# A decoder layer on one core: eight raw weight buffers instead of four, and steps put in another order at the front's end and in the tail

## The chip, the core and the metric

The kernel runs on one core of a Trainium2 chip. A core has five engines, each with its own queue: TensorE (PE in the profile, its weight loads PEld), VectorE (DVE), ScalarE (ACT), GpSimd (POOL) and SyncE (SP), which here issues nearly all transfers from the chip's memory (HBM) to the core's on-chip memory. Matrix products end in eight banks of PSUM. An engine works its queue off in order and waits on semaphores for what another engine or a transfer has to deliver. The metric is the device time of one execution in microseconds; lower is better.

## The reference

One decoder layer for 256 tokens of width 1024, in float32:

```
n = rmsnorm(h);  proj = n @ W_in            # 5136 columns, split into 10 parts
o_a = gla(q, k, v, log_a)                   # gated linear attention, chunks of 64
y_a = (rmsnorm(o_a) * silu(g_r)) @ W_branch_a
o_b = diff_attention(rope(q), rope(k), v)   # causal, 4 heads, two softmaxes each
y_b = (rmsnorm(o_b) * (1 - lambda_init)) @ W_branch_b
h1 = h + (sigmoid(gate_a) * y_a + sigmoid(gate_b) * y_b) @ W_out
n2 = rmsnorm(h1)
top-1 of 4 groups, then top-2 of its 8 experts (router in full precision)
h2 = h1 + sum_e comb[:, e] * ((silu(n2 @ w_gate[e]) * (n2 @ w_up[e])) @ w_down[e])
e = rmsnorm(p @ w_ple)
out = rmsnorm(h2 + sigmoid(h2 @ w_ple_gate) * e)
```

There are 32 experts with three matrices of 1 MB each, so some 100 MB of the 138 MB that the kernel reads are expert weights.

## The kernel before

**Front.** All products with w_in, the branch matrices and w_out run as a list `units` of 114 units. A unit takes one raw weight tile of 128 x 512, splits it into a high and a low part (`part` and `split`, lines 346 and 244: ACT copies the high part, DVE subtracts to get the low one) and multiplies both 128-token halves with three products each (`mm3`, line 411). Units 0 to 7 are q and k of the linear attention, 8 and 9 the forget gate, 10 to 17 its v, then the differential attention's q, k, v, the output gate, 32 units of branch gates, 16 of the branches (82 to 97) and 16 of w_out (98 to 113). `run` (line 383) emits a unit, keeps three units split ahead and five loaded ahead: `raw_load` (line 340) issues the load of unit i into one of four buffers tagged w_raw, on SP.

Between the units two lanes of generators (`back`, `side`) emit the attention steps: `step` (line 361) advances one, and what the generator yields is the number of units until its next step. `head_steps` (line 750) scales a branch's heads, waits by a yield, and transposes them to oT on TensorE (pt is named poT); `merge_steps` (line 805) does the same for the merged branches (pmT). Before unit 78 all that is left in the lanes is emitted at once (lines 787 to 790).

**Slots.** 22 slots of 1 MB, and a 23rd when the front's weight pool is closed, hold first the front's tensors and then expert weights. `ring` (line 200) is the order in which they come free, `tiles` (line 202) the order in which expert weights are loaded: of each group q of four experts eight tiles "gu" (gate and up) and four "d" (down), at the end quarters of the last down matrices ("dq") and of w_ple_gate ("wg"). In the front every third unit issues half a tile, if the list `fill` holds a free slot; at first `NFREE` = 11 do. `refill` (line 217) issues the rest, in the queue order of SP: after the last unit five tiles and a half that is left over, then one for the 23rd slot, then four each time four are used up.

**End of the front.** The last three w_out units are held until their three weight tiles are there (`out_unit`, line 853). `h1_half` adds the residual on DVE, `h1_turn` transposes h1 on TensorE for the router, `h1_square` sums squares on ACT and uses the product's bank as scratch, `logits` (line 895) multiplies with the router weights into a bank that is freed by the first square. `inv_root` (line 954) makes the norm's factor: a sum on DVE and a power on POOL. `route` (line 992) then runs on DVE for both token halves, and `gather` (line 982) collects the tokens of each expert by products with a one-hot matrix (pxg).

**Experts and tail.** `experts_in(q)` (line 1140) gathers, multiplies with gate and up (tile ph), gates, transposes; down products and the scatter back into the accumulators yp follow. The last two groups' down products are done in quarters of 256 columns (`down`, `scatter`, lines 1254 and 1279), interleaved with the final gate's products (pg), which need h2 = hn in the transposed form (`turn`). hn starts as yp + h1, four adds on DVE at lines 1271 to 1274, behind the last group. The end is a list of steps written out by hand (lines 1383 to 1386): sigmoid on ACT, product and add on DVE, squares, the final norm's `root`, and four stores.

The wrapper `Ordered` (line 50) keeps an engine's instructions in program order where its flag is on; in the expert part the framework may reorder them.

Of the kernel before, what the change touches and what calls it, by code (L numbers as in the profile page):

```python
# [20 lines left out]
P = 128  # L21
# [12 lines left out]
NFREE = NSLOT - 11  # L34
# [29 lines left out]
def kernel(  # L64
# [38 lines left out]
    def col(t, a):  # L103
        return a[:, t:t + 1]
# [95 lines left out]
    ring = list(range(11, NSLOT)) + [2, 5, 3, 6, 8, 7, 4, 9, 10, 1, 0, NSLOT]  # L200
# [138 lines left out]

    def raw_load(i):  # L340
        if i < len(units) and i not in raws and i not in parts and i >= state["i"]:
            src, kc, n, name = units[i][0]
            raws[i] = wst.tile([P, kc, n], F32, tag="w_raw", name=f"{name}_r", bufs=4)
            Y.dma_start(raws[i], src.rearrange("(k p) n -> p k n", p=P))

    def part(i):
        if i < len(units) and i not in parts:
            src, kc, n, name = units[i][0]
            if i == 0:
                x_parts(0, [0])  # L350
            elif i < KC:
                x_parts(i)
            if units[i][3]:
                parts[i] = [wst.tile([P, kc, n], F32R, tag=f"w_{c}", name=f"{name}_{c}") for c in "hl"]
                split(parts[i][0], parts[i][1], raws.pop(i), None)
            else:
                parts[i] = raws.pop(i)
            if i == 0:
                x_parts(0, [1])
# [23 lines left out]
    def run(upto):  # L383
        while state["i"] < upto:
            i = state["i"]
            for a in range(5):
                raw_load(i + a)
                if a < 3:
                    part(i + a)
# [3 lines left out]
            raw_load(i + 5)  # L393
# [356 lines left out]
    def head_steps(b):  # L750
# [9 lines left out]
        if b == 0:  # L760
            yield 5
        oT = slot((7, 4)[b], [2, 4, T], F32R, f"oT{b}")
        oTs[b] = oT
        for t in range(NT):
# [5 lines left out]
            yield 2 - b  # L770
# [34 lines left out]
    def merge_steps(n):  # L805
# [5 lines left out]
        yield 3  # L811
# [14 lines left out]
    accw, held = [], []  # L826

# [22 lines left out]
    def out_mm(t, n, k, ws):  # L850
        mm3(accw[t][n], [a[:, k, t * P:(t + 1) * P] for a in mT], [w_[:, 0, :] for w_ in ws], k == 0, k == KC - 1)

    def out_unit(k, n):
        def f(ws):
# [18 lines left out]
            out_mm(1, 1, 6, w61)  # L873
            for n_ in range(2):
                h1_turn(0, n_)
            out_mm(1, 1, 7, w71)
            h1_half(1, 1)
            for n_ in range(2):
                h1_square(0, n_)
# [6 lines left out]

    state["quiet"] = len(units) - 8
# [3 lines left out]
    refill(2 + len(fill))  # L891
# [9 lines left out]
    for n in range(2):  # L901
        h1_turn(1, n)
    logits(0, 1)
    h1_square(1, 0)
    h1_square(1, 1)
    logits(1, 0)
# [43 lines left out]
    rstd2 = wk.tile([P, NT], F32, name="rstd2")  # L950
    mhalf = wk.tile([P, 1], F32, name="mhalf")
    Q.memset(mhalf, -0.5)

    def inv_root(y, ms):

        V.scalar_tensor_tensor(y, ms[0], EPS, ms[1], ALU.add, ALU.add)
        Q.tensor_tensor(y, y, mhalf, ALU.pow)

    for t in range(NT):
        inv_root(col(t, rstd2), (ss2[:, t, 0:1], ss2[:, t, 1:2]))  # L960
# [31 lines left out]
    def route(t):  # L992
# [20 lines left out]
        for i, _ in enumerate(gather(0, t)):  # L1013
            if i:
                yield from until("pk1")
# [124 lines left out]
    def experts_in(q):  # L1140
# [30 lines left out]
        for h in range(2):  # L1171
            last = q == NQ - 1 and h == 1
            E.on = E.on or last
# [73 lines left out]
    last_ys = []  # L1247
# [20 lines left out]

    first = tiles.index(("gu", NQ - 1, 6))
    hn = slot(slot_of(first - 4), [NT, D], F32, "hn")  # L1270
    for t in range(NT):
        for n in range(2):
            cs = slice(n * 512, (n + 1) * 512)
            V.tensor_tensor(by_rows(hn[:, t, cs]), by_rows(yp[t][n]), by_runs(t, n), ALU.add)
# [108 lines left out]
    for f, *a in ((sig, b00), (mul, b00), (sig, b01), (add, b00), (mul, b01), (sig, b10), (square, b00), (normed, 0, 0, 512), (add, b01),  # L1383
                  (mul, b10), (sig, h0), (sig, h1), (normed, 0, 512, 1024), (square, b01), (add, b10), (mul, h0), (square, b10),
                  (add, h0), (root, 0), (mul, h1), (scaled, 0, 0, 512), (square, h0), (add, h1), (scaled, 0, 512, 1024), (square_v, h1),
                  (root, 1), (normed, 1, 0, 512, V), (finished, 1, 512, 768), (scaled, 1, 0, 512, A), (finished, 1, 768, 1024)):
# [32 lines left out]
```

## Time and profile before

| what | value |
|---|---|
| median of 3 runs | 448.23 us (448.19 to 448.48) |
| the profiled execution's own time | 448.06 us |
| its span from the first to the last instruction | 446.5 us |
| TensorE busy | 407.3 us (91%) |
| DVE, ACT, POOL busy | 218.3, 154.5, 35.7 us |
| transfers | 139.18 MB, mean 312 GB/s |

How to read it: an engine's row gives busy time; what counts is where it waits, and for whom. A line of a timeline shows start, duration, engine, line, operation, what is written <- what is read, sizes, count, and in brackets how long the engine stood idle before it and who ended that. Nearly every operation goes through the wrapper's line 58, so tiles and not lines tell them apart; buffer numbers are left out of tile names. A matmul that is listed with 0.6 us for two may overlap its neighbours: the pace is read from start to start. SPq lines are transfers issued by SP; their duration includes SP's own waiting between the merged ones.

### The profile page before, as it was taken

What the parts mean: (1) busy time and instruction counts of PE and PEld (TensorE: products, weight loads), DVE (VectorE), ACT (ScalarE), POOL (GpSimd) and SP (SyncE); (2) the same over time, 40 slices, a digit from 0 to 9 for tenths busy, and PEclk for the clock granted to TensorE, in tenths of its full rate; (3) what the DMA queues carried; (4) which work ended last, traced back from release to release, by engine and by line L of the source; (5) the groups of instructions that cost most, each with busy time, mean ns of one, the idle gap of its engine ahead of it and who ended that gap; (6) DMA issues with size and microseconds to landing.
All of it is one profiled execution on the core that took longest, in us unless ns stands there. A gap on an engine that the chain in (4) does not pass through costs nothing. (4 is left out here: it accounts for less than half of the span.)

```text
span 446.5 us, 7553 instructions
## 1 busy us (share of the span) xinstructions
PE 407.3 (91%) x2876; PEld 273.0 (61%) x2876; DVE 218.3 (49%) x478; ACT 154.5 (35%) x335; POOL 35.7 (8%) x83
## 2 busy tenths in 40 slices
PE   7999999999998999988898988899997998869990
PEld 4767777778786877868545545445263266436670
DVE  4657765896978468656403121222141163073545
ACT  5748645588555535436000000000010100042334
POOL 7200004000160000001000000000000000000003
PEclk9999999999999999999989999989899799988996
DMA  7688875678878888889599999999999999999502
GB/s 222 175 265 277 286 241 156 226 244 283 289 226 275 278 302 274 287 333 349 188 426 418 420 415 420 418 421 419 418 420 420 423 419 420 382 370 364 206 0 94
DMA packets 47214, 139.18 MB, mean 312 GB/s; under 512 B 7282, under 2 KB 17222, under 8 KB 38088
## 3 DMA queue, kind: packets, MB, share of 16 engines
q1 hardware_dynamic: 46872, 138.35, 84.5%
q8 instruction: 23, 0.38, 0.4%
q10 hardware_dynamic: 144, 0.26, 0.2%
q14 instruction: 15, 0.12, 0.1%
q0 software_dynamic: 160, 0.07, 0.1%
HBM read 137.62 MB, written 1.05 MB: 311 GB/s over the span
## 5 line engine op out<-in xcount | busy, mean ns | idle before, releaser
L58 PE MATMUL ph<-wt,xg 128*32 128x256 f32 x1024 | 61.4, 380 | 1.4 <-DMA wt<-in_w_up_dram 1.4
L58 PEld LDWEIGHTS ph<-wt,xg 128*32 128x32 f32 x1024 | 34.4, 110 | 24.5 <-DMA wt<-in_w_up_dram 1.8
L58 ACT ACTIVATE misc<-ph 128x256 f32<-128x256 f32 x8 | 3.1, 384 | 114.6 <-PE ph L58 114.6
L58 PE MATMUL sg<-sg_h,xT 128*128 128x512 f32 x128 | 40.3, 396 | 0.0
L58 PE MATMUL py<-wt,misc 128*32 128x512 f32 x192 | 32.6, 714 | 6.7 <-DVE misc L58 4.7
L58 PEld LDWEIGHTS pxg<-pq,xh 128*128 128x128 f32 x256 | 29.6, 192 | 5.2 <-issue 2.7
L58 PE MATMUL pxg<-pq,xh 128*128 128x128 f32 x256 | 30.4, 276 | 1.9 <-PEq L1061 1.6
L58 DVE TENSOR_TENSOR sg_l<-sg_r,sg_h 128x512 fp32r<-128x512 f32 x32 | 23.5, 736 | 10.5 <-ACT sg_h L58 10.4
L58 PE MATMUL pg<-wg,h2T 128*128 128x512 f32 x96 | 27.2, 420 | 0.7 <-ACT h2T L58 0.7
L58 PEld LDWEIGHTS sg<-sg_h,xT 128*128 128x128 f32 x128 | 23.4, 188 | 4.3
L58 PE MATMUL sg<-sg_l,xT 128*128 128x512 f32 x64 | 25.3, 395 | 0.1
L58 ACT ACTIVATE sg_h<-sg_r 128x512 fp32r<-128x512 f32 x32 | 19.9, 628 | 14.6 <-DMA sg_r<-in_w_in_dram 8.9
L58 PEld LDWEIGHTS py<-wt,misc 128*32 128x32 f32 x192 | 7.4, 124 | 26.8 <-issue 16.0
L58 DVE TENSOR_TENSOR xg<-pxg,g_exp 128x512 f32<-128x512 f32 x16 | 11.0, 690 | 23.0 <-PE pxg L58 22.7
L58 DVE SCALAR_TENSOR_TENSOR misc<-df,wr 128x128 f32<-128x128 bf16 x16 | 3.9, 288 | 37.1 <-PE phT L58 37.0
L58 PEld LDWEIGHTS pg<-wg,h2T 128*128 128x128 f32 x96 | 17.5, 198 | 7.2 <-issue 2.9
L58 PE MATMUL wo<-wo_h,mT 128*128 128x512 f32 x64 | 20.2, 396 | 1.3 <-ACT wo_h L58 1.3
L58 POOL TENSOR_TENSOR sgs<-hn,rows 128x512 f32<-128x512 f32 x2 | 2.5, 1282 | 229.3 <-DVE hn L58 229.3
L58 PE MATMUL y<-y_h,oT 128*128 128x512 f32 x64 | 20.1, 395 | 0.0
L58 DVE TENSOR_TENSOR wo_l<-wo_r,wo_h 128x512 fp32r<-128x512 f32 x16 | 11.0, 691 | 10.2 <-ACT wo_h L58 9.8
L58 DVE TENSOR_TENSOR y_l<-y_r,y_h 128x512 fp32r<-128x512 f32 x16 | 10.9, 691 | 8.3 <-ACT y_h L58 8.3
L58 PE MATMUL y<-late,misc 128*128 128x512 f32 x32 | 14.9, 608 | 0.0
(312 smaller groups left out, 738.7 us busy)
## 6 DMA issues: line engine op xcount, KB each, us to landing
wt<-in_w_up_dram SPq DMA_DIRECT2D x27, 1024.0 KB, 19.2
wt<-in_w_gate_dram SPq DMA_DIRECT2D x24, 1024.0 KB, 19.8
wt<-in_w_down_dram SPq DMA_DIRECT2D x20, 1024.0 KB, 19.8
wt<-in_w_down_dram SPq DMA_DIRECT2D x24, 512.0 KB, 9.3
wt<-in_w_gate_dram SPq DMA_DIRECT2D x16, 512.0 KB, 5.2
sg_r<-in_w_in_dram SPq DMA_DIRECT2D x32, 256.0 KB, 3.2
wt<-in_w_up_dram SPq DMA_DIRECT2D x10, 512.0 KB, 4.5
wo_r<-in_w_out_dram SPq DMA_DIRECT2D x16, 256.0 KB, 4.7
```

Of the source, the lines that this page charges most:

```text
L58: ins = getattr(self.engine, name)(*args, **kwargs)
```

## The change

1. **Raw buffers.** Slot 20 (NSLOT - 2) becomes four more raw buffers for the whole front (`more`); units alternate in fours between the w_raw tiles and the four pieces of `more`. `run` loads eight units ahead. NFREE falls to 10, slot 20 moves to the end of the ring in front of slots 1 and 0, and the closing refill grows by one. The last unit's split parts go into w_raw buffers.
2. **Yields.** Between scaling and transposes `head_steps` waits five units for branch 0 as before and three for branch 1 (none before); `merge_steps` waits five and four instead of three.
3. **End of the front.** The square of (0,0) is emitted ahead of the transposes of h1, that of (0,1) at the end of the held units; the norm's factor for each half is made inside the router's products (`norm2`), in pieces of sinT and cosT, and no longer behind them. In `route` four gather products of the first half are emitted ahead of the second half's rank, not two.
4. **Tail.** The four adds of hn move into `experts_in` of the last group, before the second half of its products (`own_order`).
5. **Last steps.** The final norm's gain product for rows 128 to 255, columns 0 to 511, moves from DVE (behind the second root) to POOL (before the first root); the first root goes ahead of an add, and the scalings of the first half go behind the square of h0.

```diff
-NFREE = NSLOT - 11
+NFREE = NSLOT - 12
-    ring = list(range(11, NSLOT)) + [2, 5, 3, 6, 8, 7, 4, 9, 10, 1, 0, NSLOT]
+    ring = list(range(11, NSLOT - 2)) + [NSLOT - 1, 2, 5, 3, 6, 8, 7, 4, 9, 10, NSLOT - 2, 1, 0, NSLOT]
...
+    more = slot(NSLOT - 2, [4, 512], F32, "more_r")
+
     def raw_load(i):
...
-            raws[i] = wst.tile([P, kc, n], F32, tag="w_raw", name=f"{name}_r", bufs=4)
+
+            raws[i] = wst.tile([P, kc, n], F32, tag="w_raw", name=f"{name}_r", bufs=4) if (i + 2) // 4 % 2 else \
+                more[:, (i + 2) % 4, :].rearrange("p (k n) -> p k n", k=kc)
             Y.dma_start(raws[i], src.rearrange("(k p) n -> p k n", p=P))
...
-                parts[i] = [wst.tile([P, kc, n], F32R, tag=f"w_{c}", name=f"{name}_{c}") for c in "hl"]
+                tag, bufs = ("w_raw",) * 2 if i == state.get("last") else ("w_h", "w_l"), 4 if i == state.get("last") else None
+                parts[i] = [wst.tile([P, kc, n], F32R, tag=tag[c], name=f"{name}_{'hl'[c]}", bufs=bufs) for c in range(2)]
...
-            for a in range(5):
+            for a in range(8):
                 raw_load(i + a)
...
-            raw_load(i + 5)
+            raw_load(i + 8)
...
-        if b == 0:
-            yield 5
+        yield (5, 3)[b]
...
-            yield 2 - b
+            yield 2
...
-        yield 3
+        yield 5 - n
...
+    rstd2, mhalf = sinT[:, 0, 0:2], cosT[:, 0, 0:1]
+    Q.memset(mhalf, -0.5)
...
+    def norm2(t):
+        inv_root(col(t, rstd2), (ss2[:, t, 0:1], ss2[:, t, 1:2]))
...
             out_mm(1, 1, 6, w61)
+            h1_square(0, 0)
             for n_ in range(2):
                 h1_turn(0, n_)
             out_mm(1, 1, 7, w71)
             h1_half(1, 1)
-            for n_ in range(2):
-                h1_square(0, n_)
+            h1_square(0, 1)
...
-    refill(2 + len(fill))
+    refill(3 + len(fill))
...
     logits(0, 0)
-    for n in range(2):
-        h1_turn(1, n)
+    h1_turn(1, 0)
+    norm2(0)
+    h1_turn(1, 1)
     logits(0, 1)
     h1_square(1, 0)
     h1_square(1, 1)
+    norm2(1)
...
-    for t in range(NT):
-        inv_root(col(t, rstd2), (ss2[:, t, 0:1], ss2[:, t, 1:2]))
...
         for i, _ in enumerate(gather(0, t)):
-            if i:
+            if i > 2:
                 yield from until("pk1")
...
+            if last:
+                own_order()
             E.on = E.on or last
...
+    def own_order():
+
+        hn_.append(slot(slot_of(first - 4), [NT, D], F32, "hn"))
+        for t in range(NT):
+            for n in range(2):
+                cs = slice(n * 512, (n + 1) * 512)
+                V.tensor_tensor(by_rows(hn_[0][:, t, cs]), by_rows(yp[t][n]), by_runs(t, n), ALU.add)
...
-                  (add, h0), (root, 0), (mul, h1), (scaled, 0, 0, 512), (square, h0), (add, h1), (scaled, 0, 512, 1024), (square_v, h1),
-                  (root, 1), (normed, 1, 0, 512, V), (finished, 1, 512, 768), (scaled, 1, 0, 512, A), (finished, 1, 768, 1024)):
+                  (normed, 1, 0, 512), (root, 0), (add, h0), (mul, h1), (square, h0), (add, h1), (scaled, 0, 0, 512), (square_v, h1),
+                  (root, 1), (scaled, 0, 512, 1024), (finished, 1, 512, 768), (scaled, 1, 0, 512, A), (finished, 1, 768, 1024)):
```

More of the change, by code (lines that the diff above doesn't have):

```diff
@@ L826, with inv_root @@
     accw, held = [], []
+    rstd2, mhalf = sinT[:, 0, 0:2], cosT[:, 0, 0:1]
+    Q.memset(mhalf, -0.5)
+    def inv_root(y, ms):
+        V.scalar_tensor_tensor(y, ms[0], EPS, ms[1], ALU.add, ALU.add)
+        Q.tensor_tensor(y, y, mhalf, ALU.pow)
+    def norm2(t):
+        inv_root(col(t, rstd2), (ss2[:, t, 0:1], ss2[:, t, 1:2]))
     ss2 = cst.tile([P, NT, 2], F32, name="ss2")
@@ L885 @@
                           (lambda: fill.extend(range(2))) if (k, n) == (1, 1) else None, True))
+    state["last"] = len(units) - 1
     state["quiet"] = len(units) - 8
@@ L949 @@
     rk = wk.tile([P, NT, NE], F32, name="rk")
[L950 to L957, printed above, removed]
-    for t in range(NT):
-        inv_root(col(t, rstd2), (ss2[:, t, 0:1], ss2[:, t, 1:2]))
     def sm(shape, name, dt=F32):
@@ L1246 @@
         wsl[q] = wk.tile([P, 1], F32, name=f"wsl{q}")
-    last_ys = []
+    last_ys, hn_ = [], []
+    first = tiles.index(("gu", NQ - 1, 6))
+    def own_order():
[4 more added lines that the diff above has]
+                V.tensor_tensor(by_rows(hn_[0][:, t, cs]), by_rows(yp[t][n]), by_runs(t, n), ALU.add)
     def outs_of(c, i):
@@ L1265 @@
         experts_in(q)
[L1269 to L1274, printed above, removed]
+    hn = hn_[0]
     V.on = A.on = E.on = Q.on = True
```

## The prediction

> **What bounds the kernel now.** I read the page first, then the engines' busy times by window, the chain of waits, the queue's and the engines' timelines. On the page (40 slices of 11.16 us) TensorE is the busy engine from the first slice to the last, while the transfers are not full until slice 20.
>
> ```profile
> PE   7999999999998999988898988899997998869990
> ...
> DMA  7688875678878888889599999999999999999502
> ```
>
> Windows cut at the seam show it sharper (columns: length, then busy us and instructions of PE, weight load, DVE, ACT, POOL; TensorE clock, DMA share, GB/s):
>
> ```profile
> 214.00:217.00 3.00, 3.00 (x63) 1.80 (x59) 0.77 (x4) 0.00 (x0) 0.00 (x0) 1.00 0.02 5
> 217.00:388.00 171.00, 154.40 (x1470) 82.24 (x1464) 41.00 (x105) 9.03 (x21) 0.00 (x0) 0.95 1.01 414
> ```
>
> Until 217 us TensorE sets the pace; all 23 slots are then full and the queue stands empty for 3 us. From 217 to 388 the transfers are at a share of 1.01, 414 GB/s. What opens that stream is one event, the end of the first half of expert group 0's products, which frees four slots:
>
> ```profile
> 213.29 7.11 PE L58 MATMUL ph<-wt,xg 128*32 128x256 f32 x128
> ```
>
> ```profile
> 217.39 3.35 SPq L58 DMA_DIRECT2D wt<-in_w_gate_dram  x4
> ```
>
> The chain of waits ends so:
>
> ```profile
> 367.12 19.95 DMA wt<-in_w_up_dram
> ...
> 387.11 2.99 PE ph L58 x25
> ...
> 429.93 6.44 PE pg L58 x28
> ```
>
> The last expert tile lands at 387.07 (367.12 + 19.95); behind it TensorE works through the tail to 436.4. So the time is: front on TensorE to 217, a stream of fixed bytes, a tail on TensorE. A microsecond taken from the front moves the stream and everything behind it, if the same number of tiles is loaded when it opens. An idle engine in the front costs nothing unless TensorE waits for it.
>
> **The raw buffers.** Four more buffers let each raw load go out eight units ahead instead of five, and wait for a split that is long done. Five pays in the front where a load is late:
>
> ```profile
> 25.00 0.63 ACT L58 ACTIVATE gv_h<-gv_r 128x512 fp32r<-128x512 f32 x1 [3.73 <-DMA gv_r<-in_w_in_dram]
> ```
>
> ```profile
> 23.71 0.62 PE L58 MATMUL gv<-gv_h,xT 128*128 128x512 f32 x2
> ...
> 24.40 0.61 PE L58 MATMUL gv<-gv_h,xT 128*128 128x512 f32 x2
> ...
> 27.44 1.03 PE L58 MATMUL pl<-tmp 128*128 128x256 f32 x4
> ...
> 35.72 0.63 PE L58 MATMUL gv<-gv_h,xT 128*128 128x512 f32 x2
> ```
>
> Three products (half a unit) take 24.40 - 23.71 = 0.69. From 24.40 to 35.72 stand 11 halves, 7.6 us, and the four products of pl, at most 1.0; 11.3 passed, so 2.7 were lost behind late loads. A load eight units ahead has 8 x 1.38 = 11 us; the page's median landing of a gate load is 3.2 us:
>
> ```profile
> sg_r<-in_w_in_dram SPq DMA_DIRECT2D x32, 256.0 KB, 3.2
> ```
>
> I take all 2.7. On SP the small loads (gains, bias, lambdas) and the half tiles now stand behind three more raw loads each; none of those waits for a running product after the first units, so nothing queues longer. The price is a slot: tile 10 and those behind it get their slot one place earlier in the ring, and at unit 98 the list of free slots is empty, so one half tile slips to unit 101 and 32 halves instead of 33 go out in the run. The closing refill makes up for it: six whole tiles (16 to 21) where five and a half went before. On SP it now follows the last raw load about three units sooner, so tiles 16 to 18 start some 4 us earlier. Tile 19 waits on SP for the last split out of the new slot; only tiles 20 and 21 queue behind it, and these wait for the last w_out product anyway. Seven tiles at 414 GB/s are 17.7 us from about unit 106 on, done before the first four slots come free. The count at the seam is again 23: cost 0, or up to one tile, 2.5 us, if that cover fails.
>
> **More products ahead of transposes.**
>
> ```profile
> 137.40 0.63 PE L58 MATMUL poT<-ident,osl 128*128 128x128 f32 x4 [0.82 <-DVE osl L58]
> ...
> 140.18 0.66 PE L58 MATMUL poT<-ident,osl 128*128 128x128 f32 x4 [0.77 <-DVE osl L58]
> ...
> 163.84 0.40 PE L58 MATMUL y<-y_l,oT 128*128 128x512 f32 x1
> ...
> 166.82 0.63 PE L58 MATMUL pmT<-ident,sg 128*128 128x128 f32 x4 [0.69 <-DVE sg L58]
> ...
> 168.96 0.62 PE L58 MATMUL y<-y_h,oT 128*128 128x512 f32 x2
> ```
>
> The attention head's two transposes wait 0.82 + 0.77 = 1.6 us for the scaling on DVE. With three more units between them the scaling is over: -1.6. By the yields the second transpose then falls to the flush after unit 77, one unit behind the first; its result is first needed at unit 86, so nothing waits. From 163.84 to 168.96 lie one product (0.23), four halves (2.8) and a transpose (0.4): 5.12 - 3.4 = 1.7 lost, 0.7 of it the merge, the rest raw loads that came late to DVE's queue. Two more units for merge 0 and eight buffers take it: -1.7. Merge 0 ends after unit 96 and is used from 98; merge 1 after 104 and from 106, one unit of 1.38 us of cover in each; if a split is late there, up to 0.6 comes back.
>
> **The end of the front.**
>
> ```profile
> 193.68 0.62 PE L58 MATMUL wo<-wo_h,mT 128*128 128x512 f32 x2
> ...
> 196.64 0.73 PE L58 MATMUL wo<-wo_h,mT 128*128 128x512 f32 x2 [1.26 <-ACT wo_h L58]
> ...
> 201.80 1.05 PE L58 MATMUL pr<-wr,h1T 128*128 128x40 f32 x8 [0.70 <-issue]
> ```
>
> ```profile
> 195.96 0.63 ACT L58 ACTIVATE wo_h<-wo_r 128x512 fp32r<-128x512 f32 x1 [2.56 <-DMA wo_r<-in_w_out_dram]
> ...
> 200.97 0.61 ACT L58 ACTIVATE wo<-xh 128x512 f32<-128x512 f32 x1
> ```
>
> ```profile
> 201.13 1.04 DVE L58 TENSOR_TENSOR xh<-wo,xh 128x512 f32<-128x512 f32 x1 [0.91 <-PE wo L58]
> ...
> 205.38 0.26 DVE L58 SCALAR_TENSOR_TENSOR lg<-pr,rstd,brt 128x40 f32<-128x40 f32 x1
> ```
>
> From the first held product (193.68) to the first routing step (205.38) go 11.7 us. The last w_out load costs TensorE 1.26; the logits' bank is freed only by the square at 200.97, which costs 0.70. Both go: that load is eight ahead, and the square of (0,0) now stands in front of the copies on ACT, ready once its add is done. At least 1.96. Laid out anew: six groups of three products at 0.69 (4.1), two transposes at poT's 0.63 (1.3), four logits and one more transpose (1.1), then ACT alone, a copy and two squares with their sums (0.6 and twice 0.8, my estimate from the 0.61), and the norm step: 8.9, and 8.2 if the transposes overlap their neighbours. The last add (1.04) lies beside the logits. The gain is 2.8 to 3.5; I take 3.0. On POOL the two powers now precede the small masks, which the rank product needs somewhere in the 3.6 us between this step and the gather. With two more gather products ahead of the second rank product, TensorE fills a wait there:
>
> ```profile
> 208.94 0.68 PE L58 MATMUL pxg<-pq,xh 128*128 128x128 f32 x4 [0.27 <-DVE r_em L58]
> ```
>
> Of 0.27 here I take 0.2, since DVE's second one-hot still has to come.
>
> **The tail.**
>
> ```profile
> 394.24 0.38 ACT L58 ACTIVATE ys_last<-pyq 128x256 fp32r<-128x256 f32 x1 [0.69 <-PE pyq L58]
> ```
>
> ```profile
> 392.74 3.95 DVE L58 TENSOR_TENSOR hn<-y,xh 128x512 f32<-128x512 f32 x4
> 396.60 0.42 DVE L58 TENSOR_TENSOR ys_last<-pyq,ys_last 128x256 fp32r<-128x256 f32 x1
> ```
>
> The four adds of hn hold DVE until 396.6, while ACT's half is ready at 394.62; the subtraction and the products behind it wait 2.0 us. The adds move to the last half of group 7, where they wait on DVE for the slot of one of that group's gate tiles; behind them queues only the group's gated product, not due before the last products end at 390.1. -2.0. If they land just ahead of that product instead, 3.95 returns and the tail is 2 slower. Late next would be the last weights: the page's DMA digits end in slice 37 (a 5, 413 to 424 us), over 12 us before TensorE's last product at 436.4, so I give nothing back.
>
> At the very end:
>
> ```profile
> 438.87 0.55 POOL L58 TENSOR_TENSOR ro<-ro,mhalf 128x1 f32<-128x1 f32 x1 [0.93 <-DVE ro L58]
> 441.04 0.93 POOL L58 TENSOR_TENSOR ro<-ro,mhalf 128x1 f32<-128x1 f32 x1 [1.62 <-DVE ro L58]
> ```
>
> ```profile
> 440.88 0.69 DVE L58 TENSOR_TENSOR sgs<-hn,rows 128x512 f32<-128x512 f32 x1
> ```
>
> The product moves from DVE to POOL, and the second power, 0.93 beside that DVE product, should take the 0.55 of the first: 0.4. On ACT a square of the second root no longer stands behind the first scaling, which waits for the first power's end at 439.4: 0.4 more, an estimate. Together -0.8; the two scaled halves go to the output queue some 0.4 later, ahead of the last stores. POOL's product delays the first root by some 0.4, off the end. Bounds -1.2 and +0.3. The Trainium skill ("SBUF — State Buffer", section "Summary: rules for kernel authors") says that a GpSimd operation reading SBUF and a VectorE one with two SBUF inputs block each other, the second waiting for the first. By it the first root may wait for a square on DVE and the gain here would be about 0.4; the 0.93 beside the 0.69 agrees with it.
>
> **The sum.** -2.7 - 1.6 - 1.7 - 3.0 - 0.2 = -9.2 for the front, -2.0 and -0.8 behind: -12.0. The profiled execution took 448.06 us (span 446.5), the median of the runs shown is 448.23, 0.17 above: 448.23 - 12.0 = 436.2.
>
> **Rivals.** First, the clock in the tail:
>
> ```profile
> 400.00:404.00 4.00, 3.72 (x20) 1.70 (x21) 1.82 (x2) 0.37 (x2) 0.00 (x0) 0.50 1.06 376
> ```
>
> ```profile
> 401.93 1.87 PE pyq L58 x16
> ...
> 406.77 1.00 PE pyq L58 x16
> ```
>
> ```profile
> 220.00:230.00 10.00, 7.88 (x47) 2.37 (x40) 2.70 (x7) 0.98 (x2) 0.00 (x0) 0.83 1.01 425
> ```
>
> After a sparse stretch TensorE runs at 0.50; sixteen products take 1.87 instead of 1.00, and a slow stretch of some 5 us costs about 2.5 (an estimate from this ratio). If the shorter wait keeps the clock up, the time is 436.2 - 2.5 = 433.7. Against it: at 220 to 230, waits not much longer than those that remain also drop it (0.83 on the mean). The Trainium skill ("TensorE: Matmul & The Clock Gate", section "Part 1: The HAM clock gate") puts the fall after one idle window of about 3.4 us that runs free of the program; these rows agree, and it leaves the outcome open.
>
> Second, DVE takes over. TensorE's waits were also DVE's time to catch up:
>
> ```profile
> 138.17 1.23 ACT L58 ACTIVATE sg_h<-sg_r 128x512 fp32r<-128x512 f32 x2 [3.18 <-DMA sg_r<-in_w_in_dram]
> ```
>
> Where DVE has no such slack, half of the front's gain returns as waits for splits: 448.23 - 4.6 - 2.8 = 440.8. For it: every scaling, split and merge there passes DVE. Against it: ACT waited 3.18 for data here, and DVE behind it, so late loads made part of the backlog.
>
> Third, the change does not reach the stream: the 23rd tile lands late and eats the shift, leaving the tail alone: 448.23 - 2.8 = 445.4. Against it are the 3 us of empty queue.
>
> Fourth, slower: the four pieces of the new slot are waited for as one tile. Then each load into it waits until the one before has landed, 4 x 3.2 = 12.8 us for eight units of 1.38 (11.0): about 1.8 us for each of 14 rounds, +25, with the gains that do not hang on the buffers some 464. It decides from a landing of 2.75 us on. Against it:
>
> ```profile
> 3.13 0.91 SPq L58 DMA_DIRECT2D xn<-in_x_dram  x2
> ```
>
> Two loads into one tile were issued back to back in 0.91 us.
>
> **How the numbers follow.** Chances: the forecast, 434 to 438, 0.52; the clock stays up 0.20; DVE 0.18; no shift 0.05; slower 0.05. The range reaches from the clock rival with the better ends of the front and the last stores (-2) to the DVE rival with 1 us of doubt in the tail: 431.7 to 441.8. It leaves out the last two cases. A measurement of this kernel tells apart about 0.2%, 0.9 us. Faster by more 0.94, within 0.01, slower 0.05.
>
> **What would show it.** In the changed profile: no wait of ACT for gv_r, sg_r or wo_r above 1 us; no wait before poT and pmT; the first routing step about 8.7 us after the first held product; ph of group 0 starting near 204 and the queue full from 208; the last up tile landing near 378; the subtraction of ys_last 0.4 us behind ACT's half; the last power at 0.55. It is wrong if ph starts later than 207, if the stream has gaps past its start, or if waits for DVE take the place of those for loads.

## The result, and the profile after

The changed kernel takes 435.75 us (median of four runs, 434.67 to 437.42); the kernel before 448.21 (447.92 to 448.48). The ratio is 0.9716 with an interval of 0.9689 to 0.9742: 2.8% faster. The profiled execution of the changed kernel took 436.0 us, its span is 434.4.

The page's busy tenths of TensorE and of the transfers, in 40 slices of 10.86 us:

```profile
PE   8999999999999999999898988898798999889990
...
DMA  7879974778898988896699999999999999999902
```

The transfers are full from the same slice on, the 21st, but it begins at 217.2 us (20 x 10.86) and not at 223.2. Windows at the seam (length, busy us and instructions of PE, weight load, DVE, ACT, POOL; clock, DMA share, GB/s):

```profile
206.00:208.00 2.00, 2.00 (x43) 1.19 (x39) 1.69 (x6) 0.00 (x0) 0.00 (x0) 1.00 0.00 0
...
210.00:380.00 170.00, 152.27 (x1458) 82.27 (x1452) 44.93 (x109) 9.01 (x21) 0.00 (x0) 0.97 1.01 416
```

The queue still runs empty before the stream opens, and the stream then holds its share of 1.01 for 170 us. So the number of tiles loaded by then did not shrink, and the shift went through to the end of the stream, as the chain of waits shows:

```profile
360.03 19.60 DMA wt<-in_w_up_dram
379.68 2.99 PE ph L58 x25
```

The last expert tile now lands at 379.63 (360.03 + 19.60) instead of 387.07: 7.4 us earlier. Behind it the tail became shorter by another 4.7.

**Where the time went, stretch by stretch.** I cut each trace at the starts of the same TensorE products: the first product of gv, of dq, of pa (the linear attention's scores, in the middle of dq), of pob (the attention heads' values), of y, of wo, of ph, the last product of ph, the last of pg. Two stretches are left out: pa to pob took 59.23 or 59.24 us in all but tail_only (59.84) and small_first (62.81), and the first to the last ph product took 177.08 to 177.24 in every kernel, which is the stream. The rows below the first two are the experiments; they are told further on.

| kernel | start to gv | gv to dq | dq to pa | pob to y | y to wo | wo to ph | ph to pg | pg to end |
|---|---|---|---|---|---|---|---|---|
| before | 22.22 | 15.12 | 10.20 | 43.47 | 24.67 | 38.39 | 45.60 | 10.50 |
| after | 23.19 | 12.39 | 11.58 | 41.01 | 22.73 | 35.68 | 40.95 | 10.49 |
| after_again | 22.26 | 12.45 | 11.39 | 41.01 | 22.75 | 35.68 | 41.03 | 10.49 |
| buf_only | 22.61 | 12.20 | 11.46 | 41.05 | 22.73 | 38.65 | 45.43 | 10.55 |
| yields_only | 22.35 | 14.90 | 10.40 | 43.59 | 25.47 | 36.02 | 45.61 | 10.48 |
| seam_only | 22.11 | 14.84 | 10.65 | 43.59 | 24.68 | 37.12 | 45.75 | 10.48 |
| tail_only | 23.15 | 15.27 | 10.91 | 44.30 | 24.73 | 37.34 | 42.48 | 10.49 |
| no_yields | 22.30 | 12.77 | 11.03 | 41.07 | 22.73 | 35.68 | 41.02 | 10.49 |
| small_first | 22.20 | 16.64 | 6.84 | 46.27 | 22.59 | 38.48 | 40.96 | 10.50 |
| small_pad | 22.25 | 12.18 | 10.20 | 40.91 | 22.74 | 35.68 | 42.55 | 10.50 |
| route_first | 22.20 | 12.33 | 11.85 | 41.04 | 22.75 | 36.60 | 42.59 | 10.50 |
| root_later | 22.52 | 12.57 | 12.33 | 41.06 | 22.75 | 35.68 | 42.49 | 10.13 |
| before_warm | 22.29 | 15.77 | 11.56 | 43.64 | 25.12 | 37.01 | 45.67 | 10.48 |
| best | 22.19 | 12.18 | 10.19 | 40.91 | 22.75 | 35.68 | 40.94 | 10.14 |

From before to after: +0.97, -2.73, +1.38, -2.46, -1.94, -2.71, then -4.65 and -0.01. Two of these the prediction had not: a loss at the very start and a loss in dq. One caution goes with such differences. In the kernels with five loads ahead two stretches scatter from profile to profile: dq to pa lies between 10.20 and 11.56, and wo to ph, where its order is that of before, between 36.02 and 38.39. The profile of before stands at the low end of the one and at the high end of the other, so what the change did to these two is taken from the experiments and from finer cuts.

The waits that answer to those shown of before, TensorE's timeline first. The heads' transposes wait no more and stand one unit apart:

```profile
139.66 0.60 PE L58 MATMUL poT<-ident,osl 128*128 128x128 f32 x4
141.49 0.60 PE L58 MATMUL poT<-ident,osl 128*128 128x128 f32 x4
...
205.80 7.11 PE L58 MATMUL ph<-wt,xg 128*32 128x256 f32 x128
```

The products of group 0 start at 205.80 instead of 213.29. In dq a wait has come that was not there before; DVE's and TensorE's timelines show it:

```profile
40.61 0.29 DVE L58 TENSOR_TENSOR tmp<-tmp 128x128 f32<-128x128 f32 x1 [3.31 <-DMA tmp<-in_lambda_k_dram]
```

```profile
44.01 0.44 PE L58 MATMUL pq<-ident,gla 128*128 128x128 f32 x2 [0.46 <-DVE gla L58]
```

DVE stands 3.31 us for the last of four small loads (lambda). Behind it in DVE's queue are a split of dq and the factor gla, for which TensorE then waits. In the kernel before the same step ran at nearly the same time:

```profile
40.27 0.29 DVE L58 TENSOR_TENSOR tmp<-tmp 128x128 f32<-128x128 f32 x1 [0.48 <-DMA dq_r<-in_w_in_dram]
```

By the step that reads it, the load is there at nearly the same time, while the products around it have come 1.8 us forward and no longer cover it. SP issued it 1.4 us earlier than before; the queue's timelines, of the changed kernel and of the kernel before:

```profile
34.91 0.43 SPq L58 DMA_DIRECT2D tmp<-in_lambda_k_dram  x1
```

```profile
36.34 0.43 SPq L58 DMA_DIRECT2D tmp<-in_lambda_k_dram  x1
```

So from issue to reader it took 5.7 us (34.91 to 40.61), and before at most 3.9 (36.34 to 40.27).

In the tail the wait of 2.02 us ahead of the products of pz is gone, and sixteen pyq products behind the first gate products take 1.07 us instead of 1.94. TensorE's timeline before and after:

```profile
397.08 0.62 PE L58 MATMUL pz<-ys_last,oT_last 128*128 128x256 f32 x3 [2.02 <-DVE ys_last L58]
...
401.86 1.94 PE L58 MATMUL pyq<-wt,misc 128*32 128x256 f32 x16
403.73 2.11 PE L58 MATMUL pg<-wg,h2T 128*128 128x512 f32 x5
```

```profile
387.24 1.08 PE L58 MATMUL pz<-ys_last,oT_last 128*128 128x256 f32 x4
...
390.44 0.96 PE L58 MATMUL pg<-wg,h2T 128*128 128x512 f32 x3 [0.69 <-ACT h2T L58]
391.33 1.07 PE L58 MATMUL pyq<-wt,misc 128*32 128x256 f32 x16
```

The last steps, POOL's and DVE's together:

```profile
423.32 3.86 POOL L58 TENSOR_TENSOR sgs<-hn,rows 128x512 f32<-128x512 f32 x3 [223.32 <-DVE hn L58]
...
426.09 1.11 DVE L58 SCALAR_TENSOR_TENSOR ro<-sso,sso 128x1 f32<-128x1 f32 x1
...
429.28 0.55 POOL L58 TENSOR_TENSOR ro<-ro,cosT 128x1 f32<-128x1 f32 x1 [1.46 <-DVE ro L58]
```

The first root's step on DVE took 0.15 us in the kernel before:

```profile
438.64 0.15 DVE L58 SCALAR_TENSOR_TENSOR ro<-sso,sso 128x1 f32<-128x1 f32 x1
```

Now it takes 1.11 and ends at 427.20, just when POOL's third product ends (423.32 + 3.86 = 427.18).

### The profile page after: what moved, and what is told of

Same layout as the page of the kernel before. It is cut to its first block, busy times and chain, and to the rows that moved or that the text cites. A ratio compares the mean times of both kernels' runs of the same rounds, so it can differ in the third digit from the quotient of the medians.

```text
span 434.4 us, 7552 instructions
## 1 busy us (share of the span) xinstructions
PE 401.2 (92%) x2876; PEld 275.6 (63%) x2876; DVE 219.5 (51%) x477; ACT 155.4 (36%) x335; POOL 37.1 (9%) x84
## 3 DMA queue, kind: packets, MB, share of 16 engines
HBM read 137.62 MB, written 1.05 MB: 319 GB/s over the span
## 4 chain that ended last, share of the span: by engine, by line
PE 56%; DMA 39%; DVE 2%; issue 1%; ACT 1%; POOL 0%; SPq 0%; POOLq 0%; DVEq 0%
DMA wt<-in_w_down_dram 14%; DMA wt<-in_w_up_dram 14%; PE sg L58 10%; DMA wt<-in_w_gate_dram 9%; PE y L58 6%; PE pg L58 5%; PE wo L58 5%; PE ph L58 3%; PE gqk L58 3%; PE dv L58 3%; PE dk L58 3%; PE gr L58 3%; PE pyq L58 2%; PE pxg L58 2%; DMA dq_r<-in_w_in_dram 1%; PE dq L58 1%
## 5 line engine op out<-in xcount | busy, mean ns | idle before, releaser
L58 PE MATMUL ph<-wt,xg 128*32 128x256 f32 x1024 | 62.5, 380 | 1.8 <-DMA wt<-in_w_up_dram 1.8
L58 PEld LDWEIGHTS ph<-wt,xg 128*32 128x32 f32 x1024 | 35.7, 110 | 24.8 <-DMA wt<-in_w_up_dram 3.1
L58 PE MATMUL py<-wt,misc 128*32 128x512 f32 x192 | 30.9, 656 | 7.4 <-DVE misc L58 4.7
L58 PE MATMUL pg<-wg,h2T 128*128 128x512 f32 x96 | 25.8, 404 | 0.7 <-ACT h2T L58 0.7
L58 PEld LDWEIGHTS sg<-sg_h,xT 128*128 128x128 f32 x128 | 23.4, 188 | 4.4
L58 POOL TENSOR_TENSOR sgs<-hn,rows 128x512 f32<-128x512 f32 x3 | 3.8, 1275 | 223.4 <-DVE hn L58 223.3
L58 PEld LDWEIGHTS pg<-wg,h2T 128*128 128x128 f32 x96 | 16.6, 188 | 6.4 <-issue 2.5
L58 DVE TENSOR_TENSOR sg_l<-sg_r,sg_h 128x512 fp32r<-128x512 f32 x16 | 12.6, 791 | 3.7 <-ACT sg_h L58 3.1
L58 PEld LDWEIGHTS sg<-sg_l,xT 128*128 128x128 f32 x64 | 12.0, 188 | 2.8 <-DVE sg_l L58 0.2
L58 DVE TENSOR_TENSOR sg_l<-more_r,sg_h 128x512 fp32r<-128x512 f32 x16 | 11.7, 743 | 3.9 <-ACT sg_h L58 2.8
L58 PEld LDWEIGHTS y<-y_h,oT 128*128 128x128 f32 x64 | 11.9, 188 | 2.3
```

Of the source, the lines that this page charges most:

```text
L58: ins = getattr(self.engine, name)(*args, **kwargs)
```

## The experiments

The theory after the result: eight buffers take away all waits for raw loads, those before poT and pmT among them; the reordered seam takes away what the buffers would otherwise give back there; the moved adds take 2 us from the tail and the clock the rest; the small loads and POOL's product give something back. The rival for each part is the prediction's own account of it. Each kernel's time is set against runs of the kernel before that stood beside it on the same chip: their medians were 449.37, 448.56 and 449.27 us in the three sets.

**Parts of the change alone, on the kernel before.**

buf_only takes point 1 of the change:

```
-NFREE = NSLOT - 11
+NFREE = NSLOT - 12
...
-            for a in range(5):
+            for a in range(8):
```

> The kernel before with the eight raw buffers alone (the slot taken from the ring, loads eight units ahead, the last parts in the raw buffers, one more tile in the closing refill). The terms as forecast: gv -2.7, the raw loads of the merge stretch -1.0 (1.7 less the 0.7 of the merge), the last w_out load -1.26, together 443.2 us. The rival read from the changed kernel's trace: DVE waits 3.3 us for the lambda loads, which stand on SP as late as before while the products ahead of them have come forward; then 1.4 us of the gv gain return in dq, and the time is 444.6. If the shift never reached the stream it would be 448.2.

Measured: 443.58 us, ratio 0.9885 (0.9847 to 0.9923): a gain of 5.2 us, where the forecast had 5.0 and the rival 3.6. The forecast's number is met by luck. The rival's loss is there (dq to pa 11.46), and the 1.26 of the w_out load does not reach ph; 2.4 in pob to y, which the forecast had given to the yields, make up for both. In the trace gv to dq is 2.9 shorter, pob to y 2.4, y to wo 1.9, with the yields of before. But wo to ph is not shorter (38.65 against 38.39), though the w_out products in it are, by 2.39 (23.41 against 25.80 from the first to the last). What comes forward there is lost behind, as all engines' timeline shows:

```profile
197.57 0.21 POOL L58 MEMSET onesb<- 128x128 bf16 x1 [65.86 <-DMA wt<-in_w_down_dram]
197.57 0.23 DVE L58 SCALAR_TENSOR_TENSOR rstd<-ss 128x1 f32<-128x1 f32 x2 [1.10 <-PE pr L58]
...
198.41 0.10 POOL L58 MEMSET one<- 128x1 f32 x1 [0.64 <-PE pr L58]
...
199.49 0.26 DVE L58 SCALAR_TENSOR_TENSOR lg<-pr,rstd,brt 128x40 f32<-128x40 f32 x1 [1.70 <-POOL rstd L58]
...
201.85 0.19 PE L58 MATMUL pk<-Mb,scr 128*128 128x32 bf16 x1 [2.32 <-DVE r_g L58]
```

In the order of before POOL's masks stand ahead of the norm's powers, and the first mask waits until 197.57. The profile puts that wait down to a transfer. But the norm's step on DVE, which reads only sums of squares, starts at the same 197.57, and there the profile names TensorE's products pr; so what both wait for is most likely memory that the front still holds (no run tests that). The next small step on POOL waits for pr until 198.41. The powers, whose inputs DVE gives at 197.8, come behind these steps, the routing step waits 1.70 for them, and TensorE 2.32 for the routing.

A finer cut shows the price. From the start of the last w_out product to ph it takes 12.58 or 12.59 us in the four kernels with five loads ahead and the old order, 15.24 here, and 12.26 or 12.27 in the changed kernel and in all its variants but route_first. So the seam's reordering is worth more with the buffers than without them.

yields_only takes point 2, seam_only point 3, tail_only the moved adds of point 4:

```
-        if b == 0:
-            yield 5
+        yield (5, 3)[b]
...
-            yield 2 - b
+            yield 2
...
-        yield 3
+        yield 5 - n
```

> The kernel before with the three changed yields alone. As forecast: poT -1.6 and the merge -0.7, 445.9 us, with no wait before poT and pmT. The rival: the raw loads, still five units ahead, are late again wherever TensorE now comes earlier, so that half of it or more returns as waits for gv_r, sg_r or wo_r: 447 or above.

Measured: 449.06 us, ratio 0.9999 (0.9970 to 1.0028), no change. The waits before poT and pmT are gone, and other waits stand in their place, for the splits of late loads (TensorE's timeline):

```profile
139.32 0.73 PE L58 MATMUL sg<-sg_h,xT 128*128 128x512 f32 x2 [0.91 <-ACT sg_h L58]
...
168.48 0.50 PE L58 MATMUL y<-y_l,oT 128*128 128x512 f32 x1 [1.34 <-DVE y_l L58]
```

The rival was right.

```
+            h1_square(0, 0)
             for n_ in range(2):
                 h1_turn(0, n_)
...
-    for n in range(2):
-        h1_turn(1, n)
+    h1_turn(1, 0)
+    norm2(0)
+    h1_turn(1, 1)
```

> The kernel before with the reordered end of the front and the gather alone (squares ahead of the copies, norm steps between the turns, three products of the gather ahead of the second rank product). The wait of 1.26 for the last w_out load stays. As forecast: 3.0 - 1.26 = 1.7 and the gather's 0.2, so 446.3 us. The rival: with the load still late, ACT reaches the squares no earlier and the routing starts where it did, 447.9 or above.

Measured: 448.23 us, ratio 0.9990 (0.9956 to 1.0023): no change that can be told, as the rival had it. In the trace wo to ph is 37.12, 1.3 below before's profile, but the other kernels with five loads ahead have 36.02 to 38.39 in this stretch without that edit, so this difference does not carry it. The finer cut tells more: from the last w_out product to ph it is 12.00 instead of 12.58 or 12.59, so the order alone is worth 0.6, where 1.9 was forecast (1.7 and 0.2).

```
             last = q == NQ - 1 and h == 1
+            if last:
+                own_order()
```

> The kernel before with the four adds of hn moved alone. As forecast: the wait of 2.02 before the last products of pz goes and nothing else, 446.2 us, the granted clock between 396 and 404 still falling to about 0.5. The rival (the clock): the shorter wait leaves TensorE busy enough, the clock stays at 1.00 through the tail, sixteen pyq products take 1.07 instead of 1.94 behind the first gate products, and the time is 443.7.

Measured: 445.03 us, ratio 0.9899 (0.9858 to 0.9939), 4.5 us; in the trace the tail is 3.1 shorter. The wait is gone (2.0), and TensorE's timeline shows a slow clock that begins later and ends earlier than before's (granted clock 0.50 from 400.1 to 403.5, before from 398.4 to 405.2):

```profile
400.12 1.65 PE L58 MATMUL pg<-wg,h2T 128*128 128x512 f32 x3 [0.69 <-ACT h2T L58]
401.70 1.92 PE L58 MATMUL pyq<-wt,misc 128*32 128x256 f32 x16
403.55 1.42 PE L58 MATMUL pg<-wg,h2T 128*128 128x512 f32 x5
```

The next five gate products take 1.42 here and 2.11 in the kernel before. So neither expectation holds whole: more than the wait went, the clock fell all the same, only for a shorter time.

The four ratios multiplied give 0.9774, the whole change has 0.9716; the 0.6% between them (2.6 us, within the intervals' reach) is where buffers and seam work together: from the last w_out product to ph the order takes back 3.0 beside the buffers (15.24 to 12.27) and 0.6 without them. The changed kernel with the old seam, which would test this directly, was not run.

**The changed kernel again, and without the yields.** after_again has no edit; no_yields puts back the three yields of before.

> The changed kernel once more, beside the three below. Its first profile had half-speed products from 7.2 to 11 us (gv 0.97 late) and no fall of the clock behind the last products of pz. If both are a matter of when a window of the clock happens to end, this execution can show another mix: the first gv product between 22.2 and 23.2 us, the tail from the last ph product to the last pg product between 41 and 44 us. If they belong to the kernel, both come again to 0.1 us.

Measured: 435.51 us, ratio 0.9723 (0.9690 to 0.9756). The start to gv is 22.26, so the +0.97 was not the change's. TensorE's timeline in the first profile of the changed kernel, then in this one:

```profile
7.15 1.22 PE L58 MATMUL gqk<-gqk_h,xT 128*128 128x512 f32 x2
...
8.59 1.05 PE L58 MATMUL gqk<-gqk_h,xT 128*128 128x512 f32 x2
```

```profile
7.17 0.73 PE L58 MATMUL gqk<-gqk_h,xT 128*128 128x512 f32 x2 [0.89 <-ACT gqk_h L58]
...
8.24 0.62 PE L58 MATMUL gqk<-gqk_h,xT 128*128 128x512 f32 x2
```

A pair takes 1.05 in one and 0.62 in the other: TensorE was at half pace until some 11 us in the first. Of 14 profiles two, after and tail_only, have this, about 0.95 us each.

> The changed kernel with the three yields of before. By the forecast the waits for the scalings come back before poT (0.8 and 0.8) and pmT (0.7): from the first pob product to the first wo product 2.3 us longer than in the changed kernel, and 2.3 us in all. The rival, from the buffers-only run: those waits came from raw loads that were late to DVE's queue, eight buffers alone remove them, and the yields are worth nothing here: 0.0 to 0.2.

Measured: 435.48 us, ratio 0.9726 (0.9690 to 0.9762), the changed kernel's time. pob to y is 41.07 and y to wo 22.73, within 0.06 of the changed kernel. The yields are worth nothing beside the buffers.

**The small loads.**

```
     def small_loads():
-        yield from wait(6)
+        yield from wait(2)
```

> The changed kernel with the nine small loads four units earlier. If DVE's wait of 3.3 us for the last lambda load is what gives back 1.4 us in dq, that wait is gone, the first pa product comes 11.6 us after the first dq product and not 11.6 later in total: the stretch from the first dq to the first pa product falls from 11.57 to 10.2, and every mark behind it comes 1.4 us earlier. If it was the late dq load itself, the stretch stays at 11.5.

Measured: 446.32 us, ratio 0.9971 (0.9936 to 1.0005): 11 us slower than the changed kernel. The small loads end the first entry of their lane; with it everything that follows in the lane came four units earlier, and the steps no longer meet their data. The largest wait is that of the rotated dq for POOL, 3.07 us (TensorE's timeline):

```profile
76.04 0.66 PE L58 MATMUL pdT<-ident,dqk 128*128 128x128 f32 x4 [3.07 <-POOL dqk L58]
```

The kernel does not answer the question: dq to pa is 6.84, since that lane came forward too. So the edit tested something else than it should. small_pad has it with four empty steps behind the loads:

```
             Y.dma_start(dst, src)
+        yield from wait(4)
```

> The changed kernel with the nine small loads four units earlier as in the run before this, and four empty steps behind them, so that every step that follows in their lane stays where it was. Then only the loads come earlier: if the wait for the last lambda load is what gives back in dq, it is gone, the stretch from the first dq product to the first pa product falls from 11.4 to 11.6 us down to about 10.2, and the end comes 1.2 to 1.4 us earlier, 434.2 us. If dq is held by something else, the stretch stays above 11 and the time near 435.5.

Measured: 434.51 us (433.56 to 434.96), ratio 0.9672 (0.9647 to 0.9697). dq to pa is 10.20, as before the change, and DVE's timeline has the step without a wait, 4.6 us earlier:

```profile
36.04 0.29 DVE L58 TENSOR_TENSOR tmp<-tmp 128x128 f32<-128x128 f32 x1
```

ph of group 0 starts at 203.19, so with this the front gains 10.1. By the traces the small loads' place in SP's queue took 1.2 to 1.4 us of the change's gain, and best, below, has the 10.2 again. The times agree with it (434.51 against 435.5), though the intervals of the ratios still overlap a little.

**The routing step.**

```
-    norm2(1)
     logits(1, 0)
...
-    for _ in range(LAG):
-        next(routes[0])
+    next(routes[0])
+    norm2(1)
+    for _ in range(LAG - 1):
+        next(routes[0])
...
-DUM1, DUM2, DUM3 = 5, 3, 0
+DUM1, DUM2, DUM3 = 2, 3, 0
```

The mask is made behind these steps as well, and the constant one earlier in a piece of cosT.

> The changed kernel with the norm step of the second half of the tokens behind the first routing step on DVE (and on POOL, with the mask and the constant one off POOL's path, and two idle products instead of five). If that norm step, which waits for the last square on ACT, holds the first routing step, it starts about 0.8 us earlier and ph of group 0 with it: from the first ph1T product to the first ph product 12.8 us instead of 13.63, and the end 0.8 earlier. The rival: the first routing step waits for that square anyway, through the memory that it takes over, and nothing moves.

Measured: 436.83 us, ratio 0.9725 (0.9678 to 0.9772), no gain; wo to ph is 0.9 longer. DVE's and TensorE's timelines:

```profile
197.30 0.26 DVE L58 SCALAR_TENSOR_TENSOR lg<-pr,sinT,brt 128x40 f32<-128x40 f32 x1 [1.12 <-PE pr L58]
```

```profile
199.66 0.19 PE L58 MATMUL pk<-Mb,scr 128*128 128x32 bf16 x1 [1.08 <-DVE r_g L58]
199.69 1.63 PE L58 MATMUL idle<-ident 128*128 128x128 f32 x6
201.11 1.91 PE L58 MATMUL pxg<-pq,xh 128*128 128x128 f32 x8
```

The routing step waits for TensorE, 5.83 us after the first transpose of h1 as in the changed kernel (5.80); the norm step held nothing. And with three idle products fewer TensorE stood 1.08 us ahead of the rank product and went on at half pace: six idle matmuls took 1.63 instead of 0.91, eight gather matmuls 1.91 instead of 1.13, 1.5 us together. Two other traces speak for the rival's cause, the memory that the step's output takes over from the front, and against the product that it reads. In buf_only the norm's step, which reads no product, is let go 2.90 us after the first transpose of h1's second half, the routing step here 2.94 after it. And in seam_only, with five loads ahead, the routing step has the product 2.72 after that transpose and does not wait. No run tests it.

**The tail and the end.**

```
-(normed, 1, 0, 512), (root, 0), (add, h0), (mul, h1),
+(normed, 1, 0, 512), (add, h0), (mul, h1), (root, 0),
```

> The changed kernel with the first root two steps later, behind the add and the product of the last two quarters. If that root's small step on DVE was held for about 0.95 us by the product that now runs on POOL, and with it everything behind it on DVE, this takes the hold off the path: from the last pg product to the start of the final two scalings 5.0 us instead of 5.58 to 5.6, 434.9 us. If the wait only moves to the next step on DVE, it stays at 5.5.

Measured: 436.60 us, ratio 0.9719 (0.9691 to 0.9748); the forecast 434.9 is not met. The profile has a slow stretch in the tail (ph to pg 42.49), and the times overlap those of the changed kernel, so I read the end alone. From the start of the last pg product to the final scalings it is 5.09 us (425.87 to 430.95) instead of 5.98, and the step on DVE takes 0.19:

```profile
425.30 3.87 POOL L58 TENSOR_TENSOR sgs<-hn,rows 128x512 f32<-128x512 f32 x3 [224.96 <-DVE hn L58]
429.00 0.19 DVE L58 SCALAR_TENSOR_TENSOR ro<-sso,sso 128x1 f32<-128x1 f32 x1
```

The hold was real: 0.9. The end of the span moves by less, 10.13 against 10.49 from the last pg product: 0.5 is given back between the final scalings and the end. The five stores now go out within 1.5 us (430.59 to 432.13) instead of 2.0; whether that is the reason was not tested.

```
-WARM = 1, 2, 2, 2
+WARM = 1, 2, 6, 2
```

> The kernel before with six idle products instead of two ahead of the last products of pz, inside the 2.02 us in which TensorE waits for DVE there. The wait stays, only the sparse stretch goes. If the tail gained more than the wait because the clock stays up, then here the sixteen pyq products behind the first gate products take 1.07 us instead of 1.94, and from the last ph product to the last pg product it is 43.1 us instead of 45.4 to 45.8, about 2.5 less in the time. If the extra gain came from somewhere else, the stretch stays at 45.6.

Measured: 449.46 us, ratio 0.9989 (0.9957 to 1.0020), no change. TensorE's timeline:

```profile
395.47 1.60 PE L58 MATMUL idle<-ident 128*128 128x128 f32 x12
...
398.48 0.61 PE L58 MATMUL pz<-ys_last,oT_last 128*128 128x256 f32 x3 [1.28 <-DVE ys_last L58]
399.87 1.11 PE L58 MATMUL ph2T<-ident,hn 128*128 128x128 f32 x4 [0.78 <-DVE hn L58]
401.68 1.65 PE L58 MATMUL pg<-wg,h2T 128*128 128x512 f32 x3 [0.69 <-ACT h2T L58]
403.25 1.94 PE L58 MATMUL pyq<-wt,misc 128*32 128x256 f32 x16
```

The idle products filled 0.7 of the wait only; 1.28, 0.78 and 0.69 remain, and the clock falls as before. This neither shows nor refutes that the wait brings the fall; it shows that 2.75 us of waits within 5 us are still enough.

best has the padded small loads, the later root, and two idle products each in the tail's waits of 0.79 and 0.69:

```
-    keep_warm(WARM[2])
+    idle = keep_warm(WARM[2])
     scatter(1, 0)
-    turn(0)
+    for then in (lambda: turn(0), lambda: None):
+        for _ in range(2):
+            E.matmul(idle[:, 0:P], ident, ident, start=True, stop=True)
+        then()
```

> The changed kernel with the padded small loads, the later first root, and two idle products each ahead of the first transposes and the first gate products of the tail, inside TensorE's waits of 0.79 and 0.69 there. If the three causes are right, the sum is 435.5 - 1.3 - 0.6 = 433.6 us, the stretch from the last ph product to the last pg product 41.0 in every run, so that the runs scatter less. If the idle products come later than the data that they wait beside, the tail is 0.1 to 0.3 longer.

Measured: 433.14 us (432.97 to 434.38, five runs), ratio 0.9657 (0.9631 to 0.9682). The interval lies below the changed kernel's, and all five runs lie below the lowest of its eight (434.67). The waits in the tail are 0.34 and 0.24, and pyq takes 1.07, so the clock stayed up in this profile. That is not yet a proof for the idle products, since it stayed up in four of the eight profiles with moved adds and without them too:

```profile
386.45 0.66 PE L58 MATMUL ph2T<-ident,hn 128*128 128x128 f32 x4 [0.34 <-DVE hn L58]
...
387.79 0.96 PE L58 MATMUL pg<-wg,h2T 128*128 128x512 f32 x3 [0.24 <-ACT h2T L58]
388.69 1.07 PE L58 MATMUL pyq<-wt,misc 128*32 128x256 f32 x16
```

## Why the prediction was right, and where it was not

Forecast 436.2, measured 435.75. That the mechanism of the stream is right, a front that ends earlier moves everything behind it, is shown; that the sum came out so closely is luck, because three errors cancel: the front gained 7.5 instead of 9.2 (1.0 of what is missing is the slow start of that one execution), the tail 4.65 instead of 2.0, the end nothing instead of 0.8.

- **gv, -2.7: right.** -2.73 in the changed kernel, -2.9 with the buffers alone.
- **SP's queue, 0: wrong.** The step was that the small loads stand behind three more raw loads each and "nothing queues longer". The last of them was issued 1.4 us earlier, yet its reader started 0.3 later, so it did take longer (5.7 us instead of at most 3.9); and the products that had covered it came earlier, which I did not ask about. The cost is 1.2 to 1.4 us, and small_pad takes it back.
- **poT, -1.6 by the yield: right in sign, wrong in its cause.** The step that failed is that the transposes wait "for the scaling on DVE" and that more units between them are what takes the wait away. DVE's timeline of before shows the second scaling behind a split that waits for ACT, which had waited 3.18 for its load:

```profile
138.84 0.69 DVE L58 TENSOR_TENSOR sg_l<-sg_r,sg_h 128x512 fp32r<-128x512 f32 x1 [0.92 <-ACT sg_h L58]
139.44 0.68 DVE L58 TENSOR_TENSOR osl<-osl,ro 128x512 f32<-128x512 f32 x1
```

  The buffers alone give pob to y 41.05, the yields alone 43.59, before 43.47. The gain was 2.46. I had the row of 3.18 on the table, for the rival on DVE, and did not follow the queue from it to poT.
- **Merge stretch, -1.7: right in size** (-1.94), all of it by the buffers; the 0.7 given to the yields belongs to them too.
- **End of the front and gather, -3.2: 0.5 short.** wo to ph -2.71. From the first held product (188.77) to the first routing step (197.97) it is 9.2, not 8.7. The terms were wrong in size: 2.39 lie in the w_out products, and the buffers alone have that (with five loads ahead these products take 23.4 to 25.8 us from profile to profile, so this part varies); behind the last of them the new order has 12.27 instead of 12.59, a gain of 0.3 where I had 1.9. What I had put at nothing is that the buffers in the old order lose 2.65 there (15.24); the order's worth is to avoid that.
- **DVE takes over (rival): no.** Apart from the load of lambda and TensorE's 0.46 behind it, no wait for DVE came into the units; the backlog was made by the loads, as argued against it.
- **No shift, and four pieces waited for as one tile (rivals): no.** The stream takes 177.1 us in both, and no product waits more than 0.2 us for a split out of the new slot. (The 464 of the last rival kept 1.0 of the merge stretch and the 1.26 of the w_out load, which hang on the buffers too; it should have been 466.)
- **Tail, -2.0, and the clock (rival, 0.20): the rival came, in about half of the profiles.** With the adds behind the last group ph to pg is 45.4 to 45.8 in all five profiles; with the adds moved it is 40.9 to 41.0 in five of nine (best among them, with its idle products) and 42.5 to 42.6 in four. The wait's 2.0 is sure; the clock gives 2.6 or 1.1 on top. I had put it against the rival that waits like those that remain also drop the clock. They still do, in four of nine, but for half as long. What decides between the two outcomes was not tested; the last section has what the traces say of it.
- **The last steps, -0.8: wrong, 0.0.** The second power is at 0.55 as forecast. But I let POOL's product delay only the first root, "off the end"; it held DVE for 0.96 us (1.11 - 0.15), and every step of the last two quarters stands behind that on DVE. The Trainium skill ("SBUF — State Buffer", section "Summary: rules for kernel authors") has the rule that I quoted, that of a GpSimd operation reading SBUF and a VectorE one with two SBUF inputs the second waits for the first; the trace agrees with it. I had applied it to a square and not to the root itself, whose two inputs of one element each are in SBUF.

Of the signs that I had named, the last power and the subtraction 0.4 behind ACT's half (387.22 and 386.80) are there; two of ACT's waits for loads above 1 us are left, 1.2 and 2.1 us (at 81.56 and 84.25, before the tiles gr of the output gate), and TensorE does not feel them; ph came at 205.8 (204.8 without the slow start), not 204, and the last tile at 379.6, not 378.

## What to carry to other kernels

When loads are late, the wait that the profile names need not be the late load: a step that stands behind a split in DVE's queue is named in its place, so follow the queue back before giving the gain to the edit at the named step. A change that moves work forward must be held against everything whose time does not move with it, small loads above all. And a step that hands work to another engine is free only if the two can run beside each other; on the last microseconds each such step is on the path.

## What the runs showed of the hardware

- A loss of pace comes in pieces. By the granted clock TensorE was at half pace for 3.4 us in the tails of tail_only (400.1 to 403.5) and small_pad (389.0 to 392.4), and for 6.8 us in the kernel before (398.4 to 405.2). The Trainium skill ("TensorE: Matmul & The Clock Gate", section "Part 1: The HAM clock gate") gives a window of about 3.4 us that runs free of the program; these lengths, one window and two, and a start that is slow in 2 of 14 profiles agree with it.
- A window need not be idle for the clock to fall. Within each trace the granted clock changes only at instants that lie whole multiples of 3.41 us apart. In the tails of the four kernels with moved adds where it fell, TensorE was busy for 1.86 to 1.94 us of the 3.41 before the fall; in the five where it did not, no window behind the last ph product has less than 2.3; with the adds behind the last group it was 0.7 to 1.4. So where those instants cut the waits goes with the outcome in all 14 profiles. This is read from the traces and not tested, and it is no threshold for the whole kernel: best had a window with 1.9 us busy (374.2 to 377.6) and no fall, route_first one with 2.4 (196.2 to 199.6) and a fall.
- At the start half pace does not show in the column of the granted clock: the window from 7 to 12 us has 1.00 in the changed kernel while pairs of products took 1.05 instead of 0.62. The packed traces tell why: the first clock event, the rise to full clock, stands at 10.9 or 11.0 us in the two slow starts and at 4.8 to 7.3 in the other twelve, and the column takes the time before it as 1.00. The pace of equal products tells it without that.
- Late loads go with scatter: over the profiles of the five kernels with five loads ahead y to wo lies between 24.67 and 25.47 us, over the nine with eight between 22.59 and 22.75.
